# Where a block-product feed-forward starts and where it turns into its down-projection: product order, early rows, spread loads

## The chip, the core and the metric

One core of a Trainium2 chip runs the whole kernel as one launch. TensorE (PE) multiplies, with weight loads shown apart (PEld); VectorE (DVE) and ScalarE (ACT) work on tiles; GpSimd (POOL) has little to do here; SyncE (SP) issues nearly all transfers (DMA). The metric is the device time of one execution in microseconds (us).

## The reference, cut to what matters

The program is three transformer blocks in a row on 1024 positions of width 1024. The change concerns the feed-forward of the second block:

```
def rms_norm(x, g):
    x32 = x.astype(jnp.float32)
    y = x32 * lax.rsqrt(jnp.mean(x32 * x32, axis=-1, keepdims=True) + EPS)
    return y * g.astype(jnp.float32)
...
        x = x + mix @ w_out[l]

        h2 = rms_norm(x, norm2_g[l]).astype(dt)
        x = x + jnp.square(jax.nn.relu(h2 @ w_ff1[l])) @ w_ff2[l]
```

`w_ff1` is 1024 x 4096 and `w_ff2` is 4096 x 1024, all in float32.

## The kernel before

Each float32 operand is split into a high part (an fp32r cast on ACT) and a low part (the rest, a subtraction on DVE), and a product of two operands is three matmuls: high by high (L286), and the two mixed ones (L287, L288). A tile has 128 partitions and mostly 512 columns.

Both matmuls of the feed-forward multiply 2 x 2 blocks with seven block products in place of eight. The left blocks are "11", "12", "22" and four sums "S1" to "S4"; the right ones "11", "21", "22" and four sums "T1" to "T4". The order of the seven products is written out by hand.

`ffn2` (L1133) is the changed stage. In its first part, for each half of the positions, the last rows of the attention's output projection are finished, `squares` and `inverse_rms` make the norm, and `blocks_of_input` (a generator, advanced twice) makes the seven right blocks: at its first step "11" and "21", at its second T1, then T2 and T3 together, then "22", then T4. Each of them needs a cast on ACT and a subtraction on DVE (L326/327 or L329/330). `spill` writes x to DRAM, and `close_x` frees its place.

In its second part a loop over p = 0 to 15 does the up-projection, 256 of the 4096 rows at a time. `blocks_of_weights` loads two weight tiles (L364, L365), forms four sums in a tile `ss` (L368 to L371) and splits them (`split_w`, L306 on ACT, L307 on DVE). `block_gemm` does the seven products, each 4 k x 3 = 12 matmuls, so 84 for one p. A squared ReLU follows (L1163 to L1165), then sums of the results (L1169 to L1172), and seven writes to DRAM (L1174).

In the third part `block_down` (L1191) does the down-projection in two groups of 8 k. It loads rows r1 and r2 of `w_ff2` (L1204, L1206), 512 KB each, and splits them or their sums into `wph` (ACT, L1243) and `wpl` (DVE, L1244); pairs of h come back from DRAM as `hr` (L1238) and are split by `split_w`. One of its products has 8 k x 4 quarters x 3 = 96 matmuls; its results are added to x (L1253), which is reloaded from DRAM ahead of it (L1182, sixteen loads of 256 KB). The order of its seven products is "11", "21", "T1", "T2", "22", "T3", "T4".

A scheduler places the instructions of this source on each engine; within an engine and within SP's queue they then run in that order. Where a function's source puts an operation is therefore not always where its engine does it.

Of the kernel before, what the change touches and what calls it, by code (L numbers as in the profile page):

```python
# [19 lines left out]
P = 128  # L20
# [154 lines left out]
class Kern:  # L175
    def __init__(self, ctx, tc, d):
# [28 lines left out]
        self.side = None  # L205
# [93 lines left out]
    def split_w(self, src):  # L299

        n = src.shape[1]
# [4 lines left out]
        self.nc.scalar.copy(hi, src)  # L306
        self.nc.vector.tensor_tensor(lo, src, hi.bitcast(F32), op=ALU.subtract)  # L307
# [6 lines left out]
    def blocks_of_input(self, pool, extra, x, gain, a, b):  # L314
# [23 lines left out]
        for k in range(4):  # L338
            t = tmp("bt", 2)
            V.tensor_tensor(t, x[k][b], x[k][a], op=ALU.subtract)  # L340
            parts("T1", t, g[k])
        t2s = []
        for k in range(4):
# [5 lines left out]
            parts("T3", t3)  # L349
            t2s.append(t2)  # L350
        for k in range(4):
            parts("22", x[k + 4][b], g[k + 4])
        for k in range(4):
            t = t2s[k]
            V.scalar_tensor_tensor(t, x[k + 4][a], g[k + 4], t, op0=ALU.mult, op1=ALU.subtract)
            parts("T4", t)
        yield B

    def blocks_of_weights(self, src1, src2, pool):
# [6 lines left out]
        s = pool.tile([P, 4, HF], F32, tag="ss", bufs=1, name="ss")  # L366
        lo, hi = slice(0, HF), slice(HF, 2 * HF)
        V.tensor_tensor(s[:, 0], r2[:, lo], r2[:, hi], op=ALU.add)  # L368
        V.tensor_tensor(s[:, 1], s[:, 0], r1[:, lo], op=ALU.subtract)
        V.tensor_tensor(s[:, 2], r1[:, hi], s[:, 1], op=ALU.subtract)  # L370
        V.tensor_tensor(s[:, 3], r1[:, lo], r2[:, lo], op=ALU.subtract)  # L371
        f = s.rearrange("p n c -> p (n c)")
        w1, w2, w3, w4 = (self.split_w(z) for z in (r1, f[:, :2 * HF], f[:, 2 * HF:], r2[:, hi]))
# [9 lines left out]
    def block_gemm(self, pool, w, B, out):  # L383

        A = self.nc.scalar

        def keep(ps, n):
            t = pool.tile([P, HF], F32, tag=n, bufs=1, name=n)
            A.copy(t, ps)
            return t  # L390
        a = self.pt("G")
        self.block_product(a, w["11"], B["11"], True, False)
        p1 = keep(a, "kp1")
        c = self.pt("G")
        self.block_product(c, w["S1"], B["T1"], True, False)
        p5 = keep(c, "kp5")
        self.block_product(a, w["S2"], B["T2"], False, False)
        u2 = keep(a, "ku2")
        b = self.pt("g")
# [791 lines left out]
    def block_down(self, pd, w, hd, x, groups, half, ha, hb, nb):  # L1191
# [5 lines left out]
        for grp in groups:  # L1197
# [5 lines left out]
            for k in ks:  # L1203
                nc.sync.dma_start(r1[k], rows(k))  # L1204
# [862 lines left out]
```

## Time and profile before

| | us |
|---|---|
| median of three runs | 3222.68 (3218.08 to 3225.14) |
| the profiled execution, whole | 3222.16 |
| its span, first to last instruction | 3220.4 |
| PE busy in it | 3098.4 (96%) |
| DVE busy in it | 2235.3 (69%) |
| ACT busy in it | 1299.7 (40%) |
| mean granted TensorE clock | 0.985 |

The span is cut by the profile into stretches and rows; a row gives the start of an instruction, its duration, its line, what it writes and reads, and in brackets how long its engine had been idle before it and what it had waited for. Matmuls overlap, so the time from one start to the next is what one costs, not its duration. The clock is given as a share: 1.00 is the upper level (2.4 GHz), 0.50 the lower (1.2 GHz). The changed stage lies between about 1176 and 1840 us of the span.

### The profile page before, as it was taken

To read this page: it belongs to the slowest core of one execution; us is meant where nothing else is said; L and a number is where in the kernel's file an instruction comes from. 1 tells how busy PE (TensorE), PEld (TensorE's weight loads), DVE (VectorE), ACT (ScalarE), POOL (GpSimd) and SP (SyncE) were. 2 spreads that over 40 slices of the span, in tenths; PEclk is the share of its full clock that TensorE was granted. 3 is DMA by queue.
4 is the path that set the end of the run, shared out by engine and by line. 5 is a ranking of instruction groups with operands and counts; after the bars stand their busy time and mean duration, and the time that the engine had idled before them with its cause. 6 is when DMAs were issued, how large, how long until landed. Compare 5 with 4: busy or idle time off the path is not lost.

```text
span 3220.4 us, 39991 instructions
## 1 busy us (share of the span) xinstructions
PE 3098.4 (96%) x14820; PEld 2523.3 (78%) x14820; DVE 2235.3 (69%) x3471; ACT 1299.7 (40%) x2060; POOL 258.1 (8%) x352
## 2 busy tenths in 40 slices
PE   8999999999879979998999999999999999999998
PEld 6787778778657768886788888777788888888887
DVE  7766774757698787775867645677676656666676
ACT  3254453332367554443434442455542222222253
POOL 0011021213251000000000022000000000000000
PEclk9999999999899989998999999999999999999999
DMA  4241432414564234446543455631131111111123
GB/s 147 63 121 58 156 115 75 125 47 111 162 173 120 75 112 153 158 155 225 188 150 109 141 146 160 201 95 55 36 97 48 45 53 53 46 46 53 46 70 101
DMA packets 184525, 345.26 MB, mean 107 GB/s; under 512 B 29221, under 2 KB 69541, under 8 KB 184202
## 3 DMA queue, kind: packets, MB, share of 16 engines
q1 hardware_dynamic: 184330, 342.71, 34.6%
q8 instruction: 117, 1.92, 0.2%
q14 instruction: 78, 0.64, 0.1%
HBM read 248.40 MB, written 90.49 MB: 105 GB/s over the span
## 4 chain that ended last, share of the span: by engine, by line
PE 51%; DMA 1%; DVE 1%; issue 0%; ACT 0%; POOL 0%; POOLq 0%; SPq 0%; DVEq 0%; ACTq 0%
PE ps_G L286 10%; PE ps_G L288 10%; PE ps_G L287 10%; PE ps_g L287 3%; PE ps_g L288 3%; PE ps_g L286 3%; PE ps_t L2022 2%; PE ps_o L1003 1%; PE ps_o L1004 1%; PE ps_s L286 1%; PE ps_t L288 1%; PE ps_t L286 1%; PE ps_t L287 1%; PE ps_s L287 1%; PE ps_s L288 1%; PE ps_o L286 0%
## 5 line engine op out<-in xcount | busy, mean ns | idle before, releaser
L286 PE MATMUL ps_G<-xsh,wh 128*128 128x512 f32 (+1 forms) x1272 | 496.8, 391 | 22.8 <-ACT wh L306 16.8
L287 PE MATMUL ps_G<-xsl,wh 128*128 128x512 f32 (+1 forms) x1272 | 496.0, 390 | 1.4 <-DVE xsl L456 1.4
L288 PE MATMUL ps_G<-xsh,wl 128*128 128x512 f32 (+1 forms) x1272 | 495.4, 390 | 0.0
L280 ACT CAST wh<-wr 128x1024 fp32r<-128x1024 f32 (+2 forms) x209 | 214.5, 1032 | 589.1 <-PE ps_G L287 325.6
L281 DVE TENSOR_TENSOR wl<-wr,wh 128x1024 fp32r<-128x1024 f32 (+2 forms) x209 | 251.4, 1208 | 87.8 <-ACT wh L280 86.7
L286 PEld LDWEIGHTS ps_G<-xsh,wh 128*128 128x128 f32 x1272 | 240.2, 189 | 71.7 <-ACT wh L306 17.1
L287 PEld LDWEIGHTS ps_G<-xsl,wh 128*128 128x128 f32 x1272 | 240.0, 189 | 51.0 <-DVE xsl L456 2.9
L288 PEld LDWEIGHTS ps_G<-xsh,wl 128*128 128x128 f32 x1272 | 239.9, 189 | 48.5 <-DVE wl L307 0.3
L286 PE MATMUL ps_g<-xsh,wh 128*128 128x512 f32 (+1 forms) x544 | 213.8, 393 | 0.0
L287 PE MATMUL ps_g<-xsl,wh 128*128 128x512 f32 (+1 forms) x544 | 212.9, 391 | 0.3 <-DVE xsl L456 0.3
L288 PE MATMUL ps_g<-xsh,wl 128*128 128x512 f32 (+1 forms) x544 | 212.5, 391 | 0.0
L1002 DVE TENSOR_TENSOR ptl<-ps_t,pth 128x512 fp32r<-128x512 f32 (+3 forms) x288 | 168.7, 618 | 62.4 <-ACT pth L1001 60.9
L1001 ACT CAST pth<-ps_t 128x512 fp32r<-128x512 f32 (+3 forms) x288 | 142.9, 536 | 139.8 <-PE ps_t L2022 75.2
L1263 DVE TENSOR_TENSOR x<-x,ps_G 128x512 f32<-128x512 f32 x141 | 95.5, 686 | 55.2 <-PE ps_G L288 54.6
L1003 PE MATMUL ps_o<-pth,vst 128*128 128x512 f32 (+3 forms) x288 | 120.4, 418 | 9.0 <-ACT pth L1001 3.2
L1004 PE MATMUL ps_o<-ptl,vst 128*128 128x512 f32 (+3 forms) x288 | 118.2, 416 | 4.5 <-DVE ptl L1002 4.0
L287 PEld LDWEIGHTS ps_g<-xsl,wh 128*128 128x128 f32 x544 | 102.6, 189 | 21.2 <-DVE xsl L456 1.3
L1722 DVE TENSOR_TENSOR fz<-ps_G,rst 128x512 f32<-128x512 f32 x70 | 48.5, 692 | 101.8 <-PE ps_G L288 101.8
L288 PEld LDWEIGHTS ps_g<-xsh,wl 128*128 128x128 f32 x544 | 102.7, 189 | 20.3 <-issue 0.6
L286 PEld LDWEIGHTS ps_g<-xsh,wh 128*128 128x128 f32 x544 | 102.7, 189 | 20.1 <-ACT xsh L451 0.3
L286 PE MATMUL ps_G<-wh,wph 128*128 128x512 f32 x256 | 101.9, 398 | 15.0 <-ACT wph L1243 15.0
L287 PE MATMUL ps_G<-ffl,wh 128*128 128x512 f32 x282 | 109.7, 389 | 0.0
(605 smaller groups left out, 7320.4 us busy)
## 6 DMA issues: line engine op xcount, KB each, us to landing
wr<-in_w_in_dram SPq DMA_DIRECT2D x65, 512.0 KB
wr<-in_w_up_dram SPq DMA_DIRECT2D x44, 512.0 KB
wr<-in_w_ff_dram SPq DMA_DIRECT2D x33, 512.0 KB
r<-in_w_ff_dram SPq DMA_DIRECT2D x32, 512.0 KB
hr<-hT SPq DMA_DIRECT2D x32, 512.0 KB
h<-fa SPq DMA_DIRECT2D x48, 256.0 KB
hT<-ft SPq DMA_DIRECT2D x48, 256.0 KB
hr<-h SPq DMA_DIRECT2D x24, 512.0 KB
```

The source lines that it names most:

```text
L280: nc.scalar.copy(hi[:, :n], raw[:, :n])
L281: nc.vector.tensor_tensor(lo[:, :n], raw[:, :n], hi[:, :n].bitcast(F32), op=ALU.subtract)
L286: mm(out, sh, mh, start=start, stop=False, **kw)
L287: mm(out, sh, ml, start=False, stop=False, **kw)
L288: mm(out, sl, mh, start=False, stop=stop, **kw)
L1001: nc.scalar.copy(hi[:, c0:], tp[:, c0:])
L1002: nc.vector.tensor_tensor(lo[:, c0:], tp[:, c0:], hi[:, c0:].bitcast(F32), op=ALU.subtract)
L1003: nc.tensor.matmul(po[:, c0:], vs, hi[:, c0:], start=start, stop=False)
L1004: nc.tensor.matmul(po[:, c0:], vs, lo[:, c0:], start=False, stop=stop)
L1263: nc.vector.tensor_tensor(x[n][hf], x[n][hf], ps, op=ALU.add)
L1722: V.tensor_tensor(z[:, 1 + hf * HF:1 + (hf + 1) * HF], ps, rst[hf], op=ALU.mult)
L2022: nc.tensor.transpose(tp[:, j * P:(j + 1) * P], pps[j][:, s * P:(s + 1) * P], self.ident)
```

## The change

The order of work at the two ends of the products is changed; the arithmetic of the blocks is the same but for the order of additions.

First, p = 0 gets a product order of its own, `first_gemm`. It begins while the norm's part still runs, adds products "11" and "12" in one accumulator, and computes "11" and "S1" a second time into others, so that "S4" can follow at once: nine products where there were seven. Its weights are loaded and summed ahead of T2, T3 and T4, with the sums in four separate tiles (`xe`). `blocks_of_input` makes "22" before T2, and each T4 next to its T2 and T3.

Second, rows r1 of k = 0 to 3 of the down-projection are loaded during the up-projection, into a pool of their own (`fp`); the source puts the loads at p = 10 to 13.

Third, in `block_down` the loads are put apart: the first two pairs of h, r1, four loads of x, then r2 two at a time with the pairs of the first product, and the other loads of x with the pairs of the second.

```
+        for k in range(4):
+            parts("22", x[k + 4][b], g[k + 4])
+        yield B
...
+            V.scalar_tensor_tensor(t2, x[k + 4][a], g[k + 4], t2, op0=ALU.mult, op1=ALU.subtract)
             t2s.append(t2)
-        for k in range(4):
-            parts("22", x[k + 4][b], g[k + 4])
-        for k in range(4):
-            t = t2s[k]
-            V.scalar_tensor_tensor(t, x[k + 4][a], g[k + 4], t, op0=ALU.mult, op1=ALU.subtract)
+        for t in t2s:
             parts("T4", t)
...
-    def blocks_of_weights(self, src1, src2, pool):
+    def blocks_of_weights(self, src1, src2, s):
...
+        s1, s2, s4, s3 = s if isinstance(s, list) else [s[:, i] for i in range(4)]
+        V.tensor_tensor(s1, r2[:, lo], r2[:, hi], op=ALU.add)
+        V.tensor_tensor(s2, s1, r1[:, lo], op=ALU.subtract)
+        V.tensor_tensor(s4, r1[:, hi], s2, op=ALU.subtract)
+        V.tensor_tensor(s3, r1[:, lo], r2[:, lo], op=ALU.subtract)
+        if isinstance(s, list):
+            pairs = [(s1, s2), (s4, s3)]
+        else:
+            f = s.rearrange("p n c -> p (n c)")
+            pairs = [(f[:, :2 * HF],), (f[:, 2 * HF:],)]
+        w1, w2, w3, w4 = (self.split_w(*z) for z in ((r1,), *pairs, (r2[:, hi],)))
...
+    def first_gemm(self, w, B):
+
+        mul = self.block_product
+        b, a, c, e = self.pt("g"), self.pt("G"), self.pt("G"), self.pt("G")
+        mul(b, w["11"], B["11"], True, False)
+        mul(b, w["12"], B["21"], False, True)
+        mul(a, w["11"], B["11"], True, False)
+        mul(c, w["S1"], B["T1"], True, False)
+        mul(e, w["S1"], B["T1"], True, True)
+        mul(c, w["S4"], B["22"], False, True)
+        pool, out = yield
+        out("11", b, None)
+        p5 = self.keep(pool, "kp5", e)
+        mul(a, w["S2"], B["T2"], False, False)
+        out("12", c, self.keep(pool, "ku2", a))
+        mul(a, w["S3"], B["T3"], False, False)
+        out("22", a, p5)
+        mul(a, w["22"], B["T4"], False, True)
+        out("21", a, None)
+        yield
...
+                    else:
+                        wts = self.blocks_of_weights(d["w_ff1"][0], d["w_ff1"][16], [new() for _ in range(4)])
                     B = next(steps)
                     self.spill(x2, xf, hf)
+                first = self.first_gemm(wts, B)
+                next(first)
+                next(steps)
             self.close_x()
+            self.fpool = tc.tile_pool(name="fp", bufs=1, side="right")
+            fp = self.fpool.__enter__()
             with tc.tile_pool(name="ff", bufs=1, side="right") as pf:
                 for p in range(16):
-                    wts = self.blocks_of_weights(d["w_ff1"][p], d["w_ff1"][p + 16], pf)
+                    if p:
+                        wts = self.blocks_of_weights(d["w_ff1"][p], d["w_ff1"][p + 16], pf.tile([P, 4, HF], F32, tag="ss", bufs=1, name="ss"))
                     h = {}
...
-                    self.block_gemm(pf, wts, B, act)
+                    if p:
+                        self.block_gemm(pf, wts, B, act)
+                    else:
+                        first.send((pf, act))
...
+                    if p >= 10 and p < 14:
+                        k = p - 10
+                        rows[0][k] = fp.tile([P, 2 * HF], F32, tag="r1", bufs=4, name="r1")
+                        nc.sync.dma_start(rows[0][k], d["w_ff2"][k * P:(k + 1) * P, :])
...
-                for n in range(KT):
-                    for hf in (ha, hb):
+                def load_x(n0, hf):
+                    for n in range(n0, n0 + 4):
                         x[n][hf] = self.h("x", "X")
                         nc.sync.dma_start(x[n][hf], xf[n * P:(n + 1) * P, hf * HF:(hf + 1) * HF])
-                self.block_down(pd, d["w_ff2"], hd, x, (range(0, 8), range(8, 16)), 16, ha, hb, 8)
+                self.block_down(pd, fp, d["w_ff2"], hd, x, load_x, (range(0, 8), range(8, 16)), 16, ha, hb, 8, rows)
...
-            r1, r2, s = {}, {}, {}
-            for k in ks:
-                r1[k], r2[k] = (pd.tile([P, 2 * HF], F32, tag=t, bufs=nb, name=t) for t in ("r1", "r2"))
+            (r1, r2), s = have, {}
+            have = [{}, {}]
+
+            def load_h(n, j):
+                raw = self.wb.tile([P, 2 * HF], F32, tag="WR", bufs=2, name="hr")
+                kk = ks[j:j + 2]
+                nc.sync.dma_start(raw[:, :len(kk) * HF].rearrange("p (k c) -> p k c", c=HF), hd[n][kk[0]:kk[0] + len(kk)].rearrange("k p c -> p k c"))
+                return raw
+            h11 = [load_h("11", j) for j in (0, 2)]
+            for o, k in enumerate(ks):
+                if k not in r1:
+                    r1[k] = (fp if o < nb // 2 else pd).tile([P, 2 * HF], F32, tag="r1", bufs=nb // 2, name="r1")
+                    nc.sync.dma_start(r1[k], rows(k))
+            if load_x is not None:
+                load_x(0, ha)
+
+            later = []
+
+            def load_r2(k):
+                r2[k] = pd.tile([P, 2 * HF], F32, tag="r2", bufs=nb, name="r2")
+                nc.sync.dma_start(r2[k], rows(k + half))
                 s[k] = pd.tile([P, HF], F32, tag="rs", bufs=nb, name="rs")
-            for k in ks:
-                nc.sync.dma_start(r1[k], rows(k))
-            for k in ks:
-                nc.sync.dma_start(r2[k], rows(k + half))
+            for j in range(0, len(ks), 2):
+                later.append(lambda kk=ks[j:j + 2]: [load_r2(k) for k in kk])
+            if load_x is not None:
+                later += [lambda a=a, f=load_x: f(*a) for a in ((4, hb), (0, hb), (4, ha))]
+                load_x = None
 
...
-                    raw = self.wb.tile([P, 2 * HF], F32, tag="WR", bufs=2, name="hr")
-                    nc.sync.dma_start(raw[:, :m].rearrange("p (k c) -> p k c", c=HF), hd[n][kk[0]:kk[0] + len(kk)].rearrange("k p c -> p k c"))
+                    raw = h11.pop(0) if h11 else load_h(n, j)
+                    if later:
+                        later.pop(0)()
```

(`load_r2` and `load_x` issue the same loads as before; `split_w` now takes several sources and splits each by itself.)

What this does to the order on an engine, at three places. On DVE, in the part before p = 0: `bt` are T blocks before their split, `ss` the sums of weights, `wl` low halves of weights. The end of T4 and the first sums in the kernel before:

```order
L355 SCALAR_TENSOR_TENSOR bt_11161<-x,vc,bt_11161 128x512
L327 TENSOR_TENSOR xe<-bt_11147,xe 128x512
L355 SCALAR_TENSOR_TENSOR bt_11175<-x,vc,bt_11175 128x512
L327 TENSOR_TENSOR xe<-bt_11161,xe 128x512
L368 TENSOR_TENSOR ss<-wr 128x512
L327 TENSOR_TENSOR xe<-bt_11175,xe 128x512
L369 TENSOR_TENSOR ss<-ss,wr 128x512
L371 TENSOR_TENSOR ss<-wr 128x512
L370 TENSOR_TENSOR ss<-wr,ss 128x512
L307 TENSOR_TENSOR wl<-ss,wh 128x1024
```

The first sums (now `xe<-wr`) and the first T2 and T3 (L353, L354) in the changed kernel:

```order
L334 SCALAR_TENSOR_TENSOR xsl<-bt,vc,xsh 128x512
L372 TENSOR_TENSOR xe<-wr 128x512
L1084 TENSOR_TENSOR xe<-xe 128x512
L373 TENSOR_TENSOR xe<-xe,wr 128x512
L1087 TENSOR_TENSOR xe<-xe 128x512
L374 TENSOR_TENSOR xe<-wr,xe 128x512
L507 TENSOR_SCALAR vn<-ps_o 128x4
L375 TENSOR_TENSOR xe<-wr 128x512
L310 TENSOR_TENSOR wl<-xe,wh 128x512 x4
L310 TENSOR_TENSOR wl<-wr,wh 128x512
L344 TENSOR_TENSOR bt<-x 128x512
L353 SCALAR_TENSOR_TENSOR bt_11264<-x,vc,bt 128x512
```

The sums and five low halves (L310) now stand ahead of the T2 and T3 blocks; behind the last T4 block stand the evictions of p = 0 and the sums of p = 1.

On SP, at the start of the down-projection: `r` are rows (L1204 and L1206 before, L1261 and L1269 after), `h` and `hT` writes of p = 15. Before:

```order
L1204 DMA r_13647<-in_w_ff_dram 128x1024
L1174 DMA hT_10763<-fa 128x512
L1174 DMA hT_10764<-ft 128x512
L1174 DMA hT_10766<-ft 128x512
L1204 DMA r_13650<-in_w_ff_dram 128x1024
L1204 DMA r_13653<-in_w_ff_dram 128x1024
L1182 DMA x<-xf 128x512 x16
L1204 DMA r_13656<-in_w_ff_dram 128x1024
L1204 DMA r_13659<-in_w_ff_dram 128x1024
L1204 DMA r_13662<-in_w_ff_dram 128x1024
L1204 DMA r_13665<-in_w_ff_dram 128x1024
L1204 DMA r_13668<-in_w_ff_dram 128x1024
```

After:

```order
L1261 DMA r_13659<-in_w_ff_dram 128x1024
L1219 DMA hT_10763<-fa 128x512
L1219 DMA hT_10764<-ft 128x512
L1219 DMA hT_10766<-ft 128x512
L1261 DMA r_13661<-in_w_ff_dram 128x1024
L1261 DMA r_13663<-in_w_ff_dram 128x1024
L1261 DMA r_13665<-in_w_ff_dram 128x1024
L1231 DMA x<-xf 128x512 x4
L1269 DMA r_13679<-in_w_ff_dram 128x1024
L1269 DMA r_13682<-in_w_ff_dram 128x1024
L1269 DMA r_13721<-in_w_ff_dram 128x1024
L1269 DMA r_13724<-in_w_ff_dram 128x1024
```

The first row of the list is now k = 4 of r1; four loads of x, not sixteen, stand behind the last r1, then eight r2, then the first pair of "21". The loads of r1 for k = 0 to 3 stand, on SP, right behind the weight loads of p = 1, the fourth behind the first write of h.

On DVE, behind the first product of the down-projection: `rs` are sums for T1, `wpl` low halves of rows. Before:

```order
L1253 TENSOR_TENSOR x<-x,ps_G 128x512
L1209 TENSOR_TENSOR rs<-r_13659,r_13660 128x512
L1253 TENSOR_TENSOR x<-x,ps_G 128x512 x3
L1244 TENSOR_TENSOR wpl<-r_13660,wph 128x512
L1209 TENSOR_TENSOR rs<-r_13662,r_13663 128x512
L1244 TENSOR_TENSOR wpl<-r_13663,wph 128x512
L1209 TENSOR_TENSOR rs<-r_13665,r_13666 128x512
L1244 TENSOR_TENSOR wpl<-r_13666,wph 128x512
L1209 TENSOR_TENSOR rs<-r_13668,r_13669 128x512
L1244 TENSOR_TENSOR wpl<-r_13669,wph 128x512
L307 TENSOR_TENSOR wl<-hr,wh 128x1024
L1244 TENSOR_TENSOR wpl<-rs,wph 128x512
```

After, where the four evictions (L1323, one row) and three such rows stand ahead of these:

```order
L1278 TENSOR_TENSOR rs<-r_13346,r_13724 128x512
L1314 TENSOR_TENSOR wpl<-r_13765,wph 128x512
L1278 TENSOR_TENSOR rs<-r_13659,r_13765 128x512
L1314 TENSOR_TENSOR wpl<-r_13768,wph 128x512
L1278 TENSOR_TENSOR rs<-r_13661,r_13768 128x512
L1314 TENSOR_TENSOR wpl<-r_13809,wph 128x512
L1278 TENSOR_TENSOR rs<-r_13663,r_13809 128x512
L1278 TENSOR_TENSOR rs<-r_13665,r_13812 128x512
L1314 TENSOR_TENSOR wpl<-r_13812,wph 128x512
L1314 TENSOR_TENSOR wpl<-rs,wph 128x512 x2
L1282 TENSOR_TENSOR rs<-rs,r_12899 128x512
L310 TENSOR_TENSOR wl<-hr,wh 128x1024
```

The low half of the first pair of "21" (`wl<-hr`) stood behind seven operations on rows once the last eviction was done; now it stands behind fifteen.

## Rows read from the trace of the kernel before

**Rows 1.** Page, part 1: busy us (share) and instructions of each engine.

```profile
PE 3098.4 (96%) x14820; PEld 2523.3 (78%) x14820; DVE 2235.3 (69%) x3471; ACT 1299.7 (40%) x2060; POOL 258.1 (8%) x352
```

**Rows 2.** Stretches: length, busy us per engine (instructions), PEclk, DMA share, GB/s.

```profile
1180.00:1196.00 16.00, 0.00 (x0) 0.00 (x0) 16.00 (x26) 9.22 (x16) 0.00 (x0) 0.61 0.00 0
1196.00:1201.00 5.00, 4.81 (x12) 3.66 (x13) 4.34 (x6) 2.74 (x5) 0.00 (x0) 0.54 0.43 113
...
1480.00:1497.00 17.00, 17.00 (x77) 14.08 (x76) 7.59 (x12) 4.66 (x8) 0.00 (x0) 1.00 0.41 147
...
1600.00:1840.00 240.00, 239.80 (x1064) 198.41 (x1063) 165.65 (x221) 105.43 (x147) 1.58 (x3) 1.00 0.41 133
```

**Rows 3.** PE timeline, stage's ends: start, us, line, operation, [idle before <-releaser].

```profile
1196.19 0.80 PE L286 MATMUL ps_G<-xsh,wh 128*128 128x512 f32 x1 [16.84 <-ACT wh L306]
1196.79 0.63 PE L287 MATMUL ps_G<-xsl,wh 128*128 128x512 f32 x1
1197.21 0.63 PE L286 MATMUL ps_G<-xe,wh 128*128 128x512 f32 x1
...
1200.63 0.40 PE L286 MATMUL ps_G<-xsh,wh 128*128 128x512 f32 x1
...
1505.79 0.80 PE L286 MATMUL ps_G<-wh,wph 128*128 128x512 f32 x1 [7.99 <-ACT wph L1243]
...
1523.83 0.80 PE L286 MATMUL ps_G<-wh,wph 128*128 128x512 f32 x1 [7.05 <-ACT wph L1243]
...
1541.27 0.50 PE L286 MATMUL ps_g<-wh,wph 128*128 128x512 f32 x1 [1.48 <-ACT wh L306]
...
1546.28 0.79 PE L287 MATMUL ps_g<-wl,wph 128*128 128x512 f32 x1 [4.28 <-DVE wl L307]
...
1551.99 0.49 PE L286 MATMUL ps_t<-wh,wph 128*128 128x512 f32 x1
```

**Rows 4.** DVE timeline before p=0's first product with a sum.

```profile
1193.17 0.69 DVE L368 TENSOR_TENSOR ss<-wr 128x512 f32<-128x512 f32 x1
1193.77 0.69 DVE L327 TENSOR_TENSOR xe<-bt,xe 128x512 fp32r<-128x512 f32 x1
...
1196.18 1.23 DVE L307 TENSOR_TENSOR wl<-ss,wh 128x1024 fp32r<-128x1024 f32 x1
...
1201.04 1.23 DVE L307 TENSOR_TENSOR wl<-wr,wh 128x1024 fp32r<-128x1024 f32 x1 [0.70 <-ACT wh L306]
```

**Rows 5.** ACT timeline at the start of the down-projection.

```profile
1505.12 0.62 ACT L1243 CAST wph<-r 128x512 fp32r<-128x512 f32 x1 [5.89 <-DMA r<-in_w_ff_dram]
1508.38 0.62 ACT L1243 CAST wph<-r 128x512 fp32r<-128x512 f32 x1 [2.64 <-DMA r<-in_w_ff_dram]
1510.13 0.62 ACT L1243 CAST wph<-r 128x512 fp32r<-128x512 f32 x1 [1.13 <-DMA r<-in_w_ff_dram]
...
1523.15 0.62 ACT L1243 CAST wph<-r 128x512 fp32r<-128x512 f32 x1 [7.96 <-DMA r<-in_w_ff_dram]
1524.44 0.62 ACT L1243 CAST wph<-r 128x512 fp32r<-128x512 f32 x1 [0.67 <-DMA r<-in_w_ff_dram]
```

**Rows 6.** SP timeline there: issues of DMAs.

```profile
1500.15 0.45 SPq L1204 DMA_DIRECT2D r<-in_w_ff_dram  x1
...
1502.86 2.16 SPq L1204 DMA_DIRECT2D r<-in_w_ff_dram  x2
1506.99 9.82 SPq L1182 DMA_DIRECT2D x<-xf  x16
```

**Rows 7.** DVE timeline, both ends of the first down product.

```profile
1497.84 0.69 DVE L1164 SCALAR_TENSOR_TENSOR fa<-ps_G,rst 128x512 f32<-128x512 f32 x1
...
1539.00 1.87 DVE L1253 TENSOR_TENSOR x<-x,ps_G 128x512 f32<-128x512 f32 x3
...
1544.41 0.68 DVE L1244 TENSOR_TENSOR wpl<-r,wph 128x512 fp32r<-128x512 f32 x1
1545.01 1.22 DVE L307 TENSOR_TENSOR wl<-hr,wh 128x1024 fp32r<-128x1024 f32 x1
```

More of the change, by code (lines that the diff above doesn't have):

```diff
@@ L204, in __init__ @@
         self.table = None
-        self.side = None
+        self.side = self.fpool = None
         self.defer = DEFER
@@ L297, in product, with split_w @@
         evict(hf, ps)
-    def split_w(self, src):
-        n = src.shape[1]
+    def split_w(self, *srcs):
+        n = sum(z.shape[1] for z in srcs)
         self.wturn += 1
@@ L305, in split_w @@
         lo = pool.tile([P, KT * P], F32R, tag="WL", name="wl")[:, :n]
-        self.nc.scalar.copy(hi, src)
-        self.nc.vector.tensor_tensor(lo, src, hi.bitcast(F32), op=ALU.subtract)
+        o = 0
+        for z in srcs:
+            c = slice(o, o + z.shape[1])
+            self.nc.scalar.copy(hi[:, c], z)
+            self.nc.vector.tensor_tensor(lo[:, c], z, hi[:, c].bitcast(F32), op=ALU.subtract)
+            o = c.stop
         return hi, lo
@@ L1039, in block1_end, with squares @@
         return x
-    def squares(self, pool, xs, extra=None):
+    def squares(self, pool, xs):
         nc = self.nc
@@ L1046, in squares @@
             o = n % 2
-            if extra is None:
+            if callable(pool):
+                s = pool()
+            else:
                 s = pool.tile([P, HF], F32, tag=f"sqa{o}" if acc[o] is None else "sq", bufs=1 if acc[o] is None else 2, name="sq")
-            else:
-                s = extra.tile([P, HF], F32, tag="E", bufs=self.n_extra, name="sq")
             nc.scalar.activation(s, x, AF.Square)
@@ L1064, in close_x @@
         del self.pools["X"]
+        if self.fpool is not None:
+            self.fpool.__exit__(None, None, None)
+            self.fpool = None
     def norm_half(self, pool, x, gain, n, hf):
@@ L1140, in ffn2 @@
         hd = {n: self.dr.tile([16, P, HF], F32, name="h" + n) for n in ("11", "21", "22", "T1", "T2", "T3", "T4")}
+        rows = [{}, {}]
         self.n_extra = 24
         with self.phase("f2", 2, G=4), tc.tile_pool(name="fe", bufs=1) as pe:
+            new = lambda: pe.tile([P, HF], F32, tag="E", bufs=self.n_extra, name="xe")
             with tc.tile_pool(name="n2", bufs=1) as pn:
@@ L1189, in ffn2, with block_down @@
         return x
-    def block_down(self, pd, w, hd, x, groups, half, ha, hb, nb):
+    def block_down(self, pd, fp, w, hd, x, load_x, groups, half, ha, hb, nb, have):
         nc = self.nc
```

40 lines of the change are left out of this document (17 added, 23 removed).

## The prediction

> **What bounds the kernel now.** The busy line of the page comes first: TensorE (PE) is busy 3098.4 us of the span [rows 1], and in the second half of the changed stage the table of stretches shows it busy 239.80 of 240 us [rows 2]. There the kernel can't gain, since every matmul stays. What can be won stands in the stage's ends, and the reader should look at the PE timeline for rows with an idle time in brackets. There are four: 16.84 us before the first product of the up-projection that needs a sum (gap A, ending 1196.19), 7.99 us at the start of the down-projection (B, 1505.79), 7.05 us within its first product (C, 1523.83), and 1.48 us, then a wait of 4.3 us two matmuls later, before its second (D, 1546.28) [rows 3]. That is 37.6 us of idle PE. Behind each the granted clock has fallen (0.54 in 1196 to 1201 [rows 2]) and matmuls start 0.42 us apart, the lower of the two levels, in place of 240/1064 = 0.226 us at the upper [rows 2, 3]. Behind A ten start so: 10 x 0.2 = 2.0 us. B and C cost about as much; D has thirteen, 2.6 us.
>
> Who is late? At A it is VectorE (DVE): 16.00 of 16 us busy while PE does nothing and DMA nothing [rows 2]. It makes all input blocks T2, T3, 22 and T4 first, and only then, at 1193.17, the sums of weights for p=0, which PE needs through ACT [rows 4]. At B and C it is DMA: ACT's casts of the rows wait for the load, 5.89, 2.64, 1.13 and 7.96 us [rows 5]. SP gives out the first row at 1500.15, two more from 1502.86, then 16 loads of x over 9.82 us, and the fourth row only behind them [rows 6]. At D it is DVE again: behind the four evictions it has a list of operations, and the low half of the first pair of "21" starts at 1545.01 [rows 7].
>
> **The down-projection (B, C, D).** All times from the end of the last up-projection product, 1497.80 (1505.79 - 7.99) [rows 3]. Rows r1 of k=0 to 3 are loaded early, and their casts lie within p=15; what then holds the first matmul is the eviction of the last bank, which DVE does from 1497.84 on in 0.69 us [rows 7]. I put the first matmul at +0.75, with no clock lost. The first product has 8 x 4 x 3 = 96 matmuls, 96 x 0.226 = 21.7 us, so it ends at +22.5 if r1 of k=4 to 7 is there in time. k=4 is needed at +0.75 + 48 x 0.226 = +11.6, k=7 at +19.7. The four loads stand where SP had its first row: the first three of before were cast at 1505.12, 1508.38 and 1510.13 [rows 5], that is +7.3, +10.6 and +12.3; the fourth follows at the spacing of queued rows, 1524.44 - 1523.15 = 1.29 us, at +13.6. All are early, k=4 by 4 us, the others by more. Before, this product ended at 1541.27 - 1.48 = 1539.79, +42.0 [rows 3]. **So far 19.5 us are won**; B and C are gone with their clock.
>
> The second product pays part of it back. Its r2 rows and its first pair of h lie behind r1 and four loads of x. From +13.6: x 2.6 us (1 MB at the same rate), eight rows 10.3, the pair 1.3: the pair has landed at +27.8, with its cast +28.9. But DVE holds it. In the new order it does four evictions (done +0.6 us behind the product), then twelve casts and sums of r2, then three operations of the T1 step, and only then the low half of the pair, 0.60 each and 1.22 [rows 7], as the order of DVE below the diff has them: 0.6 + 15 x 0.6 + 1.22 = 10.8 us, so PE goes on at 22.5 + 10.9 = +33.4. Before it went on at 1546.28 = +48.5, 6.5 us behind the first product. The wait D grows from 5.8 to nearly 11 us, and its cold clock remains. **Net: 48.5 - 33.4 = 15.1 us.** The three rows of T1 work done ahead are then missing from the next list, so nothing more is late; the other x loads, spread behind the pairs, are needed only at the evictions of products 2 to 4, 20 us or more away. Bounds: if the loads come at half the rate, the pair's cast is at 13.6 + 2 x 14.2 + 1.1 = +43 and the net is 5; if DVE gets part of its list done ahead of the evictions, D stays at 6.5 and the net is 19.5. I take 15, since both ends need something no row shows.
>
> The casts moved into p=15 (four of 0.6 us on DVE and on ACT) cost nothing: DVE had gaps there (in 1480 to 1497 it is 7.59 of 17 us busy, ACT 4.66 [rows 2]). Without that cover they would cost 2.4 us.
>
> **The first up-projection (A).** Added: "11" and "S1" of p=0 are computed twice, 24 matmuls, 24 x 0.226 = 5.4 us, and they run while PE had nothing. Moved ahead of T2 to T4 on DVE: four sums and five halves of 0.6 us and a low half of 1.13 for p=1, 6.5 us, so S1 (twice) and S4 can run from about 1180. But the same 6.5 us push T4's last low half from 1193.77 + 0.6 = 1194.4 [rows 4] to some 1201, and the evictions of p=0 and the sums of p=1 stand behind that. The gain is therefore not the gap. I laid the instructions of PE, DVE, ACT and SP out in the new order by hand, each starting when its engine and its inputs are ready, with the durations and spacings of the rows (on DVE 0.60 us from start to start, 1193.77 - 1193.17 [rows 4]). Laid out so, the kernel before resumes at 1196.6 (1196.19 in the trace), and S4 of p=1 is nearly through at 1227.8; the changed one is there at 1223.9. Of p=0 two products more than before, and of p=1 "11", are done before 1197, but S2, S3 and "22" wait 1 to 3 us each for DVE, and p=0 ends only at 1212.8, against 1196.19 + 60 x 0.226 + 2.0 = 1211.8 before. **Gain: 4 us.** Bounds: no holes in p=1 after 1212.8 would give 7 us; the lower clock during the sparse stretch, on the 36 matmuls of S2, S3 and "22", takes 36 x 0.2 = 7.2 back: -3.
>
> For that clock the rows show that it falls in each idle stretch and is back ten to thirteen matmuls after work resumes [rows 2, 3]. The Trainium skill, TensorE: Matmul & The Clock Gate, Part 1, says that the default state is throttled and sustained activity releases it; the trace agrees behind all four gaps, but no row shows a stretch in which PE is fed in pieces, as it will be from 1180 to 1212. If the pieces did not count as sustained, the term would be the -3 above instead of +4.
>
> The loads of r1 ahead (2 MB, 5.1 us at 1.29 us a row) go out behind p=1's weights, where DMA was empty (0.00 in 1180 to 1196 [rows 2]); free.
>
> **Sum:** 15 + 4 = 19 us against the profiled execution's 3222.16 us, which is 0.5 us from the median of 3222.68: 3203 us. A difference of 0.2%, 6.4 us, is about what a measurement of this kernel can tell from no change.
>
> **Rivals.** (1) *The new wait takes most of it.* DVE's list or the loads hold the second product as far back as +43 (the bound above), and A gives 0 to 4: gain 5 to 10, near 3214. For it: the list ahead of the pair grows, and r2 shares the queue with x. Against: the pair lands some 3 us before DVE wants it. (2) *The gaps go as a whole.* If DVE interleaves well and PE runs from 1180 and from +0.75 with only a short D, then 37.6 + 8 of clock - 5.4 of added work - 10 that stays = 30 us: 3192. Against: DVE has no free time to 1201 [rows 2, 4]. (3) *Slower, by the clock.* Fed in pieces, PE stays at the lower level from 1180 through p=0 and p=1. Each matmul costs 0.2 us more; to cancel 19 and lose 6.4 it takes 25.4 / 0.2 = 127 matmuls on the bound, all of p=1 and half of p=0: 3229 or more. Against: the clock came back within 13 matmuls everywhere. (4) *The rows ahead don't help*, since r1's casts or the first pairs of "11" are themselves late: then B and C stay, and D grows by 5 beside A's 4: no change, 3223.
>
> **Chances.** Forecast (gain 11 to 25) 0.62, rival 1 0.16, rival 2 0.10, rival 3 0.05, rival 4 0.07. Half of rival 1 is below 6.4 us only at its end, so I count 0.03 of it as the same. Faster 0.85, same 0.10, slower 0.05. The range reaches over the forecast and into rivals 1 and 2: 3192 to 3213.
>
> **What will show it.** Right: PE has no idle row of over 2 us between the last product of p=15 and the second of the down-projection, whose first low half comes some 11 us behind the first product, with DVE busy throughout; the first product lasts 22 us; from 1180 to 1212 PE is busy in pieces and DVE wholly. Wrong: r1 of k=4 cast later than 11.6 us after p=15 (DMA slower with the new mix), the pair cast later than its list on DVE, or a granted clock near 0.5 beyond 1215.

## The result, and the profile after

The changed kernel takes 3202.99 us (median of five runs, 3198.78 to 3206.49), beside 3225.14 us for the kernel before in the same comparison. The ratio is 0.9926, with a 95% interval from 0.9898 to 0.9954: 0.7% faster. The prediction was 3203 us. That both agree to the microsecond is chance: the five runs spread over 7.7 us, and the kernel before, from whose 3222.68 us the prediction counted, is at 3225.14 here.

A whole time hides where it went, since the program ahead of the stage, which is the same code, ends up to 9 us earlier or later from one execution to the next. So all that follows is counted within the stage, in one profiled execution of each kernel, from the last addition to x of the output projection (a DVE row) to the last one of the down-projection. These are the two rows of the kernel before:

```profile
1171.51 0.68 DVE L1292 TENSOR_TENSOR x<-x,ps_G 128x512 f32<-128x512 f32 x1
1832.39 0.68 DVE L1253 TENSOR_TENSOR x<-x,ps_G 128x512 f32<-128x512 f32 x1
```

And of the changed kernel:

```profile
1174.09 0.68 DVE L1362 TENSOR_TENSOR x<-x,ps_G 128x512 f32<-128x512 f32 x1
1815.08 0.68 DVE L1323 TENSOR_TENSOR x<-x,ps_G 128x512 f32<-128x512 f32 x1
```

660.88 us have become 640.99: 19.9 us less. Everything behind the stage takes the same (1388.0 and 1387.8 us to the end of the span).

The idle rows of PE in the stage, changed kernel (start, us, line, operation, [idle before <-releaser]), answer to [rows 3]:

```profile
1199.60 0.80 PE L286 MATMUL ps_G<-xe,wh 128*128 128x512 f32 x1 [2.50 <-ACT xe L330]
...
1204.79 0.79 PE L286 MATMUL ps_g<-xsh,wh 128*128 128x512 f32 x1 [3.25 <-DVE fa L1206]
...
1496.52 0.50 PE L286 MATMUL ps_G<-wh,wph 128*128 128x512 f32 x1 [0.79 <-DVE fa L1206]
...
1526.57 0.80 PE L286 MATMUL ps_g<-wh,wph 128*128 128x512 f32 x1 [7.96 <-ACT wh L309]
...
1530.19 0.79 PE L287 MATMUL ps_g<-wl,wph 128*128 128x512 f32 x1 [1.97 <-DVE wl L310]
```

What to see: gap A of 16.84 us is two holes of 2.50 and 3.25; B is 0.79, and it waits for the eviction; C is gone; D has grown to 7.96 and 1.97. The end of p=15 is 1496.52 - 0.79 = 1495.73, 321.64 us behind the first row of the stage (before 1497.80 - 1171.51 = 326.29). From there the first product ends at +22.88 (before +41.99), and the first low-half matmul of the second comes at +34.46 (before +48.48).

By stretches (us, then busy us and instructions of PE, PEld, DVE, ACT, POOL, the granted clock, the DMA share, GB/s), the changed kernel, beside [rows 2]:

```profile
1180.00:1197.00 17.00, 16.99 (x78) 13.26 (x76) 16.96 (x27) 11.46 (x19) 0.68 (x1) 1.00 0.21 62
1180.00:1199.00 19.00, 17.09 (x78) 13.26 (x76) 18.87 (x29) 11.52 (x20) 0.68 (x1) 1.00 0.19 55
1199.00:1211.00 12.00, 8.15 (x20) 5.78 (x21) 11.32 (x17) 8.52 (x14) 0.00 (x0) 0.57 0.64 218
...
1518.00:1531.00 13.00, 3.07 (x8) 1.74 (x7) 13.00 (x22) 8.38 (x15) 0.00 (x0) 0.72 1.02 388
```

PE now works where it had stood, without a gap up to 1197 (16.99 of 17 us), DVE is still busy throughout (18.87 of 19), and in the last row, the wait D, DVE and the DMA engines are both full. Which of the two holds the second product can't be read from this row; the experiments below ask that.

The table gives every kernel that was run. "p=15" is from the first row of the stage to the end of the up-projection; "low 21" from there to the first low-half matmul of the second down product (L287 on `ps_g`); "stage" the whole.

| kernel | p=15 | low 21 | stage |
|---|---|---|---|
| before | 326.29 | 48.48 | 660.88 |
| changed | 321.64 | 34.46 | 640.99 |
| e1, up-projection's part alone | 319.18 | 49.41 | 654.39 |
| e2, down-projection's part alone | 328.80 | 34.09 | 647.79 |
| e3, r2 two pairs later | 322.08 | 28.08 | 634.88 |
| e4, x together | 321.18 | 41.03 | 647.03 |
| e5, sums on GpSimd | 321.76 | 36.35 | 643.77 |
| e6, no rows ahead in the source | 321.25 | 35.15 | 642.37 |
| e7, old product order | 326.98 | 33.98 | 646.24 |
| e8, four more on DVE | 323.64 | 34.78 | 644.24 |
| e9, e1 and the pool | 321.23 | | |
| e11, r2 three pairs later | 321.70 | 25.59 | 630.20 |
| e12, rows in the down pool | 319.01 | 42.16 | 646.55 |

Six kernels have the first part of the changed one, and their first column runs from 321.18 to 322.08. e6 turned out to do the work of the changed kernel in all but the same order, so it can serve as a second execution of it: it differs by 0.4, 0.7 and 1.4 us in the three columns. That is the measure for the differences below.

### The profile page after: what moved, and what is told of

Read it like the earlier page. It is cut to its first block, busy times and chain, and to the rows that moved or that the text cites. A ratio compares the mean times of both kernels' runs of the same rounds, so it can differ in the third digit from the quotient of the medians.

```text
span 3202.9 us, 40059 instructions
## 1 busy us (share of the span) xinstructions
PE 3102.0 (97%) x14844; PEld 2525.3 (79%) x14844; DVE 2233.6 (70%) x3472; ACT 1298.2 (41%) x2061; POOL 257.3 (8%) x352
## 4 chain that ended last, share of the span: by engine, by line
PE 50%; DVE 1%; DMA 1%; issue 1%; ACT 0%; POOL 0%; SPq 0%; POOLq 0%; DVEq 0%; ACTq 0%
PE ps_G L287 10%; PE ps_G L288 10%; PE ps_G L286 10%; PE ps_g L287 3%; PE ps_g L286 3%; PE ps_g L288 3%; PE ps_t L2092 2%; PE ps_o L1032 1%; PE ps_o L1033 1%; PE ps_s L286 1%; PE ps_t L288 1%; PE ps_t L287 1%; PE ps_t L286 1%; PE ps_s L287 1%; PE ps_s L288 1%
## 5 line engine op out<-in xcount | busy, mean ns | idle before, releaser
L287 PE MATMUL ps_G<-xsl,wh 128*128 128x512 f32 (+1 forms) x1276 | 496.9, 389 | 1.1 <-DVE xsl L485 1.1
L287 PEld LDWEIGHTS ps_G<-xsl,wh 128*128 128x128 f32 x1276 | 240.3, 188 | 50.3 <-DVE xsl L485 2.3
L287 PE MATMUL ps_g<-xsl,wh 128*128 128x512 f32 (+1 forms) x548 | 216.9, 396 | 0.2 <-DVE xsl L485 0.2
L287 PEld LDWEIGHTS ps_g<-xsl,wh 128*128 128x128 f32 x548 | 104.7, 191 | 21.5 <-DVE xsl L485 1.2
L287 PE MATMUL ps_G<-ffl,wh 128*128 128x512 f32 x282 | 109.7, 389 | 0.0
L288 PE MATMUL ps_G<-ffh,wl 128*128 128x512 f32 x282 | 109.7, 389 | 0.0
```

The costliest lines, as they stand in the source:

```text
L287: mm(out, sh, ml, start=False, stop=False, **kw)
L288: mm(out, sl, mh, start=False, stop=stop, **kw)
```

## The experiments

### e1 and e2: the two parts apart

e1 keeps the new beginning of the up-projection and takes the loads and `block_down` of the kernel before. e2 is the other way round.

```diff
 e1, against the changed kernel
-            self.fpool = tc.tile_pool(name="fp", bufs=1, side="right")
-            fp = self.fpool.__enter__()
...
-                    if p >= 10 and p < 14:
...
+                self.block_down(pd, d["w_ff2"], hd, x, (range(0, 8), range(8, 16)), 16, ha, hb, 8)
```

> Only the first part of the change: p=0's own product order, early weights, new order of the input blocks; the down-projection loads as in the kernel before. Theory (two separate terms that add): the time from the last eviction of the output projection to the end of p=15 is shorter by 4.6 us than before, as in the changed kernel's trace, and gaps B, C and D stand as before (8, 7 and 6 us); whole time about 3225 - 5 = 3220 us. Rival (the two parts help each other, DVE backlog moved from one to the other): the first term comes out under 2 us alone.

> Only the second part: rows r1 of k=0 to 3 ahead, loads of x spread; p=0 as before. Theory: from the end of p=15 to the first low-half matmul of the second down product 34.5 us in place of 48.5, so 14 to 15 us shorter than before, gap A as before at 16.8 us; whole time about 3225 - 15 = 3210 us. Rival (the rows ahead cost p=0 and p=1 something when their weights and the rows share the queue): the stretch before gains nothing and p=0 to p=2 get holes, whole time 3213 or more.

e1: stage 654.39, 6.5 us less than before; whole time 0.9986 of before (0.9972 to 1.0000). e2: stage 647.79, 13.1 us less; 0.9950 (0.9927 to 0.9972). The sum, 19.6, is the 19.9 of both within the spread: the parts add in time, though, as the next rows show, not wait by wait.

But their first columns were not expected. With the first part alone p=15 ends at 319.18, which is 7.1 us ahead of before, not 4.6; and with the second part alone it ends at 328.80, which is 2.5 us *behind* before. Something in the second part costs the up-projection 2.5 us. e2's PE timeline (columns as above) shows it as a longer gap A and two small holes:

```profile
1199.56 0.80 PE L286 MATMUL ps_G<-xsh,wh 128*128 128x512 f32 x1 [17.74 <-ACT wh L306]
...
1207.63 0.50 PE L286 MATMUL ps_G<-xsh,wh 128*128 128x512 f32 x1 [0.83 <-ACT kp L389]
...
1214.17 0.50 PE L286 MATMUL ps_G<-xe,wh 128*128 128x512 f32 x1 [0.77 <-DVE fa L1169]
```

17.74 in place of 16.84, and 0.83 + 0.77: 2.5 us. So both theories (4.6 from the first part, and gap A as before with the second) and e1's rival (the parts help each other) were off: the first part is worth more, and the second takes some of it.

e2's rival, weights that share the queue with the rows, has a part in it here. The hole of 0.83 us waits for a copy (`kp`) that stands on ACT right behind a cast of the weights of p=1, and that cast waits for their load. The two casts, first in the kernel before, then in e2:

```profile
1199.96 1.05 ACT L306 CAST wh<-wr 128x1024 fp32r<-128x1024 f32 x1 [2.10 <-DMA wr<-in_w_ff_dram]
```

```profile
1206.05 1.05 ACT L306 CAST wh<-wr 128x1024 fp32r<-128x1024 f32 x1 [4.01 <-DMA wr<-in_w_ff_dram]
```

SP issued that load at 1196.33 and at 1199.66, so from issue to cast it took 3.6 us before and 6.4 us behind the rows. In the changed kernel the weights of p=1 are loaded earlier, ahead of the rows, and this wait does not arise.

### e9: the pool of rows without the rows

In the changed kernel the second hole of 3.25 us waits for an eviction on DVE (in e1 it is 1.25 us), and ACT's copy for p=0 waits 1.79 us for a T4 block. In e1 the same copy does not, as the ACT timelines show, first the changed kernel, then e1:

```profile
1203.98 0.59 ACT L414 COPY kp<-ps_G 128x512 f32<-128x512 f32 x1 [1.79 <-DVE xe L331]
```

```profile
1196.94 0.58 ACT L414 COPY kp<-ps_G 128x512 f32<-128x512 f32 x1 [0.51 <-ACT xe L330]
1197.42 0.59 ACT L414 COPY ku<-ps_G 128x512 f32<-128x512 f32 x1
1197.90 0.63 ACT L330 CAST xe<-bt 128x512 fp32r<-128x512 f32 x1
```

The eviction behind which the hole ends stands, in the changed kernel, after the last low half of T4; in e1 it has three of them behind it. DVE's timeline of the changed kernel:

```profile
1201.46 2.49 DVE L331 TENSOR_TENSOR xe<-bt,xe 128x512 fp32r<-128x512 f32 x4
1204.05 0.69 DVE L1206 SCALAR_TENSOR_TENSOR fa<-ps_g,rst 128x512 f32<-128x512 f32 x1
```

A copy out of an accumulator has no business with T4's sources, unless its target stands where they stood. e9 puts the pool, and no rows, into e1:

```diff
+            self.fpool = tc.tile_pool(name="fp", bufs=1, side="right")
+            fp = self.fpool.__enter__()
...
+                    if p == 13:
+                        hold = fp.tile([P, 8 * HF], F32, tag="r1", name="r1")
+                        nc.sync.dma_start(hold[:, :P], d["w_ff2"][:P, :P])
```

> The run with the first part alone, plus the pool of the rows (16 KB per partition) standing where the changed kernel has it, with one load of 64 KB at p=13 and no rows. It asks why the up-projection ends 2.5 us later when rows are loaded ahead (321.6 against 319.2 us from the last eviction of the output projection). Theory, from the trace (the copies kp and the eviction of p=0 wait for the last low half of T4, which they don't without the pool): the pool pushes the tiles of the up-projection onto the place of T4's sources, so 321.6 without any load. Rival (2 MB on the queue ahead of the weights of p=2): 319.2.

321.23 us, with 64 KB on the queue in place of 2 MB: the pool's place costs 2.1 of the 2.5 us, and the copy waits again as in the changed kernel:

```profile
1200.23 0.59 ACT L414 COPY kp<-ps_G 128x512 f32<-128x512 f32 x1 [1.79 <-DVE xe L331]
```

The hole before the first matmul of p=1 sorts the kernels in the same way: it is 1.25 us in e1 and e12, which begin with `first_gemm` and have no such pool, and 3.24 to 3.84 us in the eight kernels that have both. So it is the pool. The explanation that fits is that its 16 KB per partition push the tiles of the up-projection over the place of the first part's temporaries (`bt`), whose last reader is T4's last low half; the evictions of p=0, and with them the accumulators, wait for it. The addresses themselves were not read; the waits are what is shown. The rival, the queue, falls for the changed kernel: at most the other 0.4 us are left to it, which is within the spread. (The down-projection of e9 is disturbed by the reserved place and isn't read.)

### e7: is it the product order or the early weights?

p=0 goes back to the seven products of `block_gemm`; the weights stay early.

```diff
-                first = self.first_gemm(wts, B)
-                next(first)
                 next(steps)
...
-                    if p:
-                        self.block_gemm(pf, wts, B, act)
-                    else:
-                        first.send((pf, act))
+                    self.block_gemm(pf, wts, B, act)
```

> The changed kernel, with the weights of p=0 early and the new order of the input blocks, but p=0 in the product order of the other p: seven products, none twice, and the copies kp1, kp5 and ku2 between them. It asks what the own order of p=0 is worth. Theory: its second accumulators let S1 and S4 run without a copy, and the copies can't be made until T4's sources are free, so with the old order S2, S3, S4 and 22 (48 matmuls, 10.9 us) all stand behind that point, in place of S3 and 22: 24 x 0.2267 = 5.4 us later, 326 to 327 us from the last eviction of the output projection to the end of p=15 in place of 321.6. Rival (early weights alone do it, and 24 matmuls less are saved): 320 or less.

326.98: 5.3 us later than the changed kernel, as the theory had it. The hole is back, and its releaser is the copy:

```profile
1202.62 0.80 PE L286 MATMUL ps_G<-xe,wh 128*128 128x512 f32 x1 [15.53 <-ACT kp L414]
```

With the old order the second use of an accumulator waits for a copy whose target isn't free. Computing two products twice (24 matmuls, 5.4 us of PE time that was idle) buys the way round that copy. What early weights and input blocks are worth by themselves is read beside e2, which has the same pool, the old order and late weights: 328.80 - 326.98 = 1.8 us. The kernel before (326.29) has no such pool, so it is not the one to compare with; and the old order with early weights and without the pool was not run.

### e8: is DVE the bound there?

```diff
             parts("T3", t3)
             V.scalar_tensor_tensor(t2, x[k + 4][a], g[k + 4], t2, op0=ALU.mult, op1=ALU.subtract)
+            V.tensor_tensor(m, t2, t3, op=ALU.add)
```

> The changed kernel with four more operations of 128 x 512 on VectorE, one behind each T4 block, whose results nobody reads: 4 x 0.60 = 2.4 us of DVE work. Theory (from 1180 to 1204 DVE is the bound of the stretch, PE waits for T4's low halves and for evictions behind them): the end of p=15 comes 2.4 us later, 324.0 us from the last eviction of the output projection in place of 321.6. Rival (ACT's casts or PE are the bound there): under 0.8 us.

323.64 in place of 321.64: 2.0 of the 2.4 us arrive at the end of p=15. DVE is the bound of the stretch, nearly one to one; the missing 0.4 us are within the spread.

### e4, e3 and e11: what holds the second down product

e4 puts the twelve other loads of x back to the start; e3 and e11 hold the r2 loads back until the third or the fourth pair of the first product, so that the first pair of "21" is sent behind four or two rows of r2, not eight.

```diff
 e4
-                load_x(0, ha)
+                for a in ((0, ha), (4, hb), (0, hb), (4, ha)):
+                    load_x(*a)
+                load_x = None
 e3 (e11 has 6 in place of 4)
-                    if later:
+                    if later and (n != "11" or j >= 4):
                         later.pop(0)()
```

> The changed kernel with all sixteen loads of x at the start, behind r1, as in the kernel before; rows ahead kept. Theory: twelve loads of 256 KB more ahead of r2, 12 x 0.64 = 7.7 us, so r2's last row lands at 36 us after the end of p=15 and the second product's first low half comes at about 40 in place of 34.5; 6 us slower than the changed kernel. Rival, as the prediction had it (only DVE's list holds the product, loads are 3 us ahead of it): 3 to 5 us. Second rival (hidden anyway): 0.

> The changed kernel, but the r2 loads come two pairs later: four r2 rows, the first pair of h for product 21, then the other r2 rows with the later pairs. Theory (the second product waits for the pair to land behind eight rows, and then for DVE's list of operations on them): the pair lands 4 x 1.28 = 5.1 us earlier, the list is 4 operations in place of 15, and the first low-half matmul of product 21 comes 27 us after the end of p=15 in place of 34.5; 7 us faster than the changed kernel. Rival (the total of the loads is the bound, so that the wait only moves): product 21 begins earlier but waits again for r2 of k=4 to 7, and the net is under 2 us.

> As the run with r2 two pairs later, but three pairs later: two r2 rows, the first pair of product 21, then two rows with each further pair. Theory: the pair lands 2.6 us earlier, and on DVE its low half stands right behind the four evictions, so PE has it at 24.7 us after p=15 (28.1 there, 34.5 in the changed kernel); two us of idle PE are left, r2 of k=2 is there at 24 and needed at 29; 9 us faster than the changed kernel in the stage. Rival (k=2 to 7 land too late and PE waits within product 21): the end of product 21 moves by under 1 us against the run with two pairs.

e4: low 21 at 41.03, 6.6 us later than the changed kernel; the theory had 40. Twelve more loads of 256 KB take 12 x 0.64 = 7.7 us, and they are no longer hidden: the first r2 row is cast at +27.7 from the end of p=15, not +19.2, and DVE's list then goes at the pace at which rows arrive. So the DMA queue is nearly as close to being the bound as DVE's list: the two end within 2.4 us of each other in the changed kernel, where the cast of the pair is done at 1526.5 and DVE comes to it at 1528.91 (its timeline):

```profile
1526.51 0.68 DVE L1314 TENSOR_TENSOR wpl<-r,wph 128x512 fp32r<-128x512 f32 x1
1527.11 1.29 DVE L1314 TENSOR_TENSOR wpl<-rs,wph 128x512 fp32r<-128x512 f32 x2
1528.31 0.68 DVE L1282 TENSOR_TENSOR rs<-rs,r 128x512 f32<-128x512 f32 x1
1528.91 1.22 DVE L310 TENSOR_TENSOR wl<-hr,wh 128x1024 fp32r<-128x1024 f32 x1
```

e3: low 21 at 28.08 (expected 27), stage 6.1 us shorter than the changed kernel, whole time 0.9916 of before (0.9901 to 0.9931). e11: low 21 at 25.59 (expected 24.7), stage 10.8 us shorter than the changed kernel, and nothing is lost within the product. Its idle rows of PE in the down-projection:

```profile
1495.62 0.50 PE L286 MATMUL ps_G<-wh,wph 128*128 128x512 f32 x1 [0.79 <-DVE fa L1206]
...
1518.01 0.50 PE L286 MATMUL ps_g<-wh,wph 128*128 128x512 f32 x1 [0.30 <-ACT wh L309]
...
1520.42 0.51 PE L287 MATMUL ps_g<-wl,wph 128*128 128x512 f32 x1 [1.20 <-DVE wl L310]
```

Of D 1.5 us are left, and the clock stays up. The same stretch for which the changed kernel had 0.72 (above), in e11:

```profile
1518.00:1531.00 13.00, 11.79 (x51) 9.43 (x52) 13.00 (x21) 8.31 (x13) 0.00 (x0) 1.00 1.00 372
```

That fits the stage, which gains 10.8 us where low 21 gains 8.9: in the changed kernel some nine matmuls behind the wait run at the lower level, about 0.2 us more each. It is the same loads in another order: the pair is sent earlier, and on DVE its low half then stands right behind the four evictions, since the rows whose casts filled the list have not come yet. e11 is the best kernel of the study: 3191.4 us, 0.9883 of before (0.9859 to 0.9908).

### e5: shortening DVE's list with GpSimd

```diff
-                V.tensor_tensor(s[k], r1[k][:, hi], r2[k][:, hi], op=ALU.add)
+                nc.gpsimd.tensor_tensor(s[k], r1[k][:, hi], r2[k][:, hi], op=ALU.add)
```

> The changed kernel with the eight sums rs (r1 + r2, for T1) on GpSimd in place of DVE; loads as they are. It takes 8 x 0.60 = 4.8 us out of the list that stands on DVE ahead of the low half of product 21's first pair. In the changed kernel that pair's cast begins 29.8 us after the end of p=15 and PE has its low half at 34.5. Theory now (both hold it, the pair's landing and, 3 us behind, the list): the low half starts as soon as the cast is done, PE has it at about 32, 2.4 us earlier. Rival (the list alone, as the prediction had it): 4.8 us earlier. Second rival (GpSimd slows DVE where both read): no gain.

Neither of the two gains came, and the second rival holds; low 21 is 1.9 us later (36.35). The list on DVE is shorter by the sums that went to GpSimd and takes longer, 9.7 in place of 9.0 us from the last eviction to the low half of the pair, as the timelines of DVE and POOL show:

```profile
1523.26 2.47 DVE L1323 TENSOR_TENSOR x<-x,ps_G 128x512 f32<-128x512 f32 x4
1525.65 7.99 DVE L1314 TENSOR_TENSOR wpl<-r,wph 128x512 fp32r<-128x512 f32 x6
```

```profile
1519.79 12.70 POOL L1278 TENSOR_TENSOR rs<-r,r 128x512 f32<-128x512 f32 x8 [334.68 <-DMA r<-in_w_ff_dram]
```

Six operations take 7.99 us, 1.33 each, where one took 0.60 in the changed kernel, as long as GpSimd works beside them. The four evictions, with one operand in PSUM, run beside it too and take 2.47 us, as they do in the changed kernel. The Trainium skill, SBUF — State Buffer, section Who interferes with whom, says that a DVE instruction with two SBUF inputs contends with a GpSimd instruction that reads SBUF; both kinds here are such, and the trace agrees: 1.33 us against 0.60. So this run says nothing for or against the list, except that GpSimd is no place for it.

### e6 and e12: no rows ahead

e6 takes the loads of r1 out of the loop over p and leaves them to `block_down`, in the same pool. e12 puts them into the pool of the down-projection, and the pool of rows goes.

```diff
 e6
-                    if p >= 10 and p < 14:
-                        k = p - 10
-                        rows[0][k] = fp.tile([P, 2 * HF], F32, tag="r1", bufs=4, name="r1")
-                        nc.sync.dma_start(rows[0][k], d["w_ff2"][k * P:(k + 1) * P, :])
 e12, on top
-                    r1[k] = (fp if o < nb // 2 else pd).tile([P, 2 * HF], F32, tag="r1", bufs=nb // 2, name="r1")
+                    r1[k] = pd.tile([P, 2 * HF], F32, tag="r1", bufs=nb, name="r1")
...
-            self.fpool = tc.tile_pool(name="fp", bufs=1, side="right")
-            fp = self.fpool.__enter__()
+            fp = None
```

> The changed kernel with all eight r1 rows loaded at the start of the down-projection, in the order r1, four x, r2; nothing is loaded during the up-projection. Theory: first matmul at 9 us after p=15 in place of 0.8, first product through at 33 in place of 22.9, four rows (5.1 us) more ahead of the first pair of product 21, its low half at 43 to 45 in place of 34.5; and the time to the end of p=15 becomes 2.5 us shorter, 319.2 from the last eviction of the output projection, as in the run with the first part alone. Rival (the spread of x did most of it): low half at under 38.

> The changed kernel with all eight r1 rows in the pool of the down-projection, which opens only behind the up-projection, and no pool of rows ahead: now the early loads are truly gone (in the run without rows ahead the scheduler had still sent them early, at 1200 us, since their place was free). Theory: the end of p=15 comes at 319.2 us from the last eviction of the output projection in place of 321.6; first down matmul at 9 us behind it in place of 0.8, first product through at 33, first low half of product 21 at 44 in place of 34.5. So rows ahead are worth some 9.5 us less the 2.4 that their place costs. Rival (loads of x alone were what counted): low half at under 38.

e6 missed altogether, and not for either reason given: it is the changed kernel again (321.25 and 35.15). Its SP timeline shows why: the scheduler still sends the rows at 1200 us, as soon as their place is free, though the source has them at the start of the down-projection.

```profile
1200.40 1.28 SPq L1257 DMA_DIRECT2D r<-in_w_ff_dram  x3
```

e12 is the undoing that was meant. First matmul at +8.68 (9 expected), the first product through at +32.90 (33), low 21 at 42.16 (44), and p=15 at 319.01 (319.2). The rows ahead are worth 42.16 - 34.46 = 7.7 us at the second product, and their place costs 2.6 us (321.64 - 319.01); in the stage 5.6 us are measured (646.55 - 640.99). The rest of the 14 us at low 21, 6.3 us, is left to the other loads; e4, which undoes the spread of x alone, has 6.6.

## Why the prediction was right

**Sum.** 19 us were forecast, 19.9 measured in the stage, and that is the fair comparison (the medians, which include the program around it, are 22 us apart). The shares: 4.65 us in the up-projection (forecast 4), 15.2 in the down-projection (forecast 15; 334.59 - 319.35 us from the end of p=15 to the end of the stage).

**B and C.** As worked out: first matmul at +0.79 (0.75), first product through at +22.88 (22.5). The step on the loads was off by 1 to 2 us and covered: r1 of k=4 was cast at +9.1, not +7.3, with +11.6 needed. (The tightest row was k=5, by the prediction's own figures: there at +10.6 and needed at +14.3, 3.7 us; it was cast at +12.2.) The casts within p=15 cost nothing.

**D.** Forecast +33.4, measured +34.46, which is 11.6 us behind the first product (before 6.5; of it PE is idle for 9.9 and 5.8 us, and the prediction's "5.8 to nearly 11" mixes the two counts). The mechanism stands (fifteen operations behind the evictions, then the low half), but the cast of the pair, put at +28.9, was done only at +30.8, 2 us later. The list still ended last, by 2.4 us. The prediction's remark against rival 1, that the pair lands some 3 us before DVE wants it, was about right, and e4 shows how thin that cover is: 7.7 us of loads put back cost 6.6. The two bounds given for the net, 5 and 19.5, are both far from the 14.0 that low 21 gained; the 15.2 at the stage's end includes a shorter stretch at the lower clock behind the wait, some nine matmuls in place of thirteen.

**A.** Here the sum, 4 us for the measured 4.65, was right by luck: its steps were wrong, and their errors cancel. The layout by hand had S2, S3 and "22" wait 1 to 3 us each, p=0 through at 1212.8 (41.3 us behind the first row of the stage), and "11" of p=1 done before 1197. In the trace PE takes 93 of the 108 matmuls of p=0 without an idle row, up to 1197.1; the two holes stand behind them; p=0 is through at 1210.2, 36.1 us behind the first row, and of p=1 one single matmul is ahead, at 1204.79, since it needs the bank that the eviction of 1204.05 frees. Without the pool this beginning is worth 7.1 us (e1). That is the prediction's upper bound in number only: the bound supposed no holes in p=1, and neither kernel has any, but the changed one gained 4.65. And the step "the loads of r1 ahead go out where DMA was empty; free" is wrong in its last word: the rows ahead cost 2.5 us. Not as loads, which were what the prediction looked at, but as a pool: e9 has 2.1 of it without them. That the order of products does the work, with the pool in place, is e7; that DVE is the bound there is e8.

**The clock.** The -3, for the case that work in pieces does not hold the clock up, didn't come, but it was hardly tested: PE was not fed in pieces but ran without a gap up to 1197, at the upper level (1.00 in 1180 to 1197). The clock fell only behind the holes of 2.50 and 3.25 us (0.57 in 1199 to 1211), for some fourteen matmuls, 2.8 us. The Trainium skill, TensorE: Matmul & The Clock Gate, Part 1, says that sustained activity releases the throttle; the trace agrees, with 1.00 again in 1211 to 1220, once PE worked without a gap. That stretch is also where rival 3 would have shown itself, and it did not.

**Rivals.** That the gaps go as a whole is, for the down-projection, what e11 then does: 30.7 us in the stage. For this change the prediction put it at 0.10, and it did not come: D grew. Rival 4, that the rows ahead don't help, falls by e12: without them low 21 comes 7.7 us later.

What stays open: whether the 0.4 us that e9 leaves of the 2.5 are the load on the queue or the spread of the measurement; which tiles the pool pushes where; and the 2.5 us themselves, for which no kernel was tried that keeps the rows and gives the up-projection its old place.

## What to carry to other kernels

A pool that is opened early for a prefetch can cost the place that the next tiles would have had, and they may then wait for readers that have nothing to do with them (here 2.1 us): look for a copy or an eviction that waits on a far producer. Where loads, casts and sums for several steps share one queue and one engine, send first what the next step needs first, and only as much of the rest as the engine can take before it: e11 gains 10.8 us over the changed kernel with the same loads in another order. And a second computation of a product on an engine that stands idle can be cheaper than the copy that would save it (e7, 5.3 us). A last one is for the reading of results: a term that comes out right is no proof of its steps; the parts run one by one (e1, e2, e9) showed that 4 us here were 7 less 2.5.

## What the runs showed of the hardware that was not expected

DVE operations with two inputs in SBUF took 1.33 us in place of 0.60 while GpSimd added two tiles beside them; those with one operand in PSUM took no longer (four in 2.47 us, e5 and the changed kernel). Matmuls stayed at the upper level through holes of 0.30 and 1.20 us (e11, granted clock 1.00 in 1518 to 1531). Behind a hole of 2.50 us, with the same work before it, they were at the lower level in the changed kernel (from 1199.60 on), but still at the upper in e4 and e9, where the clock fell only behind the next hole; the stretch with the three matmuls behind the first hole in e9:

```profile
1195.00:1198.00 3.00, 1.23 (x3) 0.48 (x3) 2.32 (x5) 2.82 (x6) 0.00 (x0) 1.00 0.00 0
```

So at this length one execution of the same work loses the clock and another keeps it.
